# A hybrid state-space and attention layer on one core: turn tied, gate buffers of their own, parities alternated, merge gates loaded early

## The chip, the core and the metric

The kernel runs on one core of one Trainium2 chip. The metric is device time in microseconds (us), the time of one execution of the program on that core. Below, PE is the TensorE, PEld its weight loads, DVE the VectorE, ACT the ScalarE, POOL the GpSimd, and SP the SyncE, whose queue issues most DMAs.

## What is computed

One decoder layer on x of 512 tokens by 1024 channels, all in float32. The reference, cut to its course:

```python
h = rms_norm(x, norm_w)
u_s, z_s, q, k, v, z_a, r_s, r_a = split(h @ w_in)
y_s = s5_branch(u_s, ...)                 # diagonal complex state space, GELU, GLU with w_glu
y_s = (y_s * silu(z_s)) @ w_ssm_out
q, k = partial_rope(rms_norm(q)), partial_rope(rms_norm(k))
y_a = dilated_attention(q, k, v)          # 3 head groups, dilations 1, 4, 16; 8 heads of 64 each
y_a = (y_a * silu(z_a)) @ w_attn_out
m = sigmoid(r_s) * y_s + sigmoid(r_a) * y_a
x = x + m @ w_o
```

## The kernel before

Every large product is made of three matmuls (`mm3`, lines 107 to 110): each operand is split into a high and a low part, and high x high (L108), high x low (L109) and low x high (L110) are summed in a PSUM bank. Weights stream from DRAM: `plan` (lines 112 to 157) lists all pieces of weights in the order of use, `get_w` takes the next and has the two after it loaded; a piece is loaded by SP into `w_raw` (two buffers), ACT makes its high part `w_hi` (L93) and DVE its low part `w_lo` (L95).

The kernel is written as a program of units, in this order:

- The norm of x and its transposition into `hT_hi`, `hT_lo`; then the projections `u` (L300 to L306, L447 to L449). A unit (`cm_unit`, L180) is 24 matmuls into one bank with the tag "pj". Beside them the powers of the state matrix are made on DVE (L307 to L390) and turned by small matmuls into `AT` (L398 to L411): 16 products with the powers' real parts (i = 0), a copy of the half bank by ACT (L405), 16 products for the imaginary parts (i = 1) into the other half of the same bank, their copy, and then `fT` in a bank of its own (L409, L411). From AT come the coefficients `coef` (L253), and from these the transposed W (`w_unit`, L282) and the states X (`x_unit`, L293).
- The gates: `za_unit`, `zs_unit`, `rs_unit`, `ra_unit` (L461 to L483). Each is a projection unit whose bank ACT empties with a tanh into a tile `th` (L458, L474, L482). For rs and ra the tile is stored to DRAM by SP (`gd`, `rad`). `th` has the tag "t2k" (L88), a ring of six buffers of 128 x 512, which it shares with many others, among them the state-space branch's `ysb`, `gs`, `gq`, and later `zl`, `gsum`, `gth`, `rl`, `qsq`, `at`, `vt`, `ral` and `ob`.
- The state-space branch runs in eight groups j (L775 to L785), with the gates' units as fillers between: `ca_unit` (small matmuls cps, L683, then six operations of coefficients on DVE), `m_unit` (16 products kps, L707, each on 64 rows of the array, 16 output partitions; copies to `kt`, eight DMAs by POOL that build the Toeplitz matrix), `y_unit` (products yps, L731 and L738), `g_unit` (transposes yT, L748, GELU, split into `gT_hi`, `gT_lo`). In the kps loop gg runs from 0 to 7, the half of the rows is gg % 2, and the two products of one gg, which add up, follow each other on the same half.
- GLU (L1023 to L1033) and the branch's output projection (L1035 to L1039).
- Attention in four pairs of heads. For each pair: `qk_first` projects q and k of groups 0 and 1 (a `wide_granule`, four quarters of 24 matmuls, L794), their norm and rotation follow on DVE (L823) and POOL (L829 to L834); `qk_turn` (L836) transposes them by PE (L842, two lots of four for each group) through a bank, which ACT (L850) and DVE (L851) empty into high and low parts `qkp`. `scores` (L898) makes the softmax, `values` (L965) transposes the probabilities (L999) and multiplies by V (L985). In the loop (L1070), the granule `qk_second` of the next pair calls `mid` before each of its quarters: the turn of group 0 before quarter 1, that of group 1 before quarter 2, `values` before quarter 3 (counted from 0).
- For the last pair, units ra 3 to 7 fill instead. Then the merge (L1098 to L1110): for each of eight column blocks the gate `ral` is loaded from `rad` (L1103), 12 matmuls are made, and DVE and ACT form `mT` (L1108 to L1110). The residual x is loaded as `xr` (L1112), and two granules with w_o end the kernel.

What is written is not quite what runs: `TileContext(nc, schedule_with_timeline_sim=True)` (L1144) puts the instructions of each engine into an order of its own when the program is built, by its reckoning of when each is ready and by their order in the program; it also places all waits. On the chip each engine then goes through its list in order. So a statement that is moved, or a buffer that is added, can shift the order elsewhere. PSUM is divided into three banks "pj" and five "g" in the first part and four "pj", three "g" and one "o" from L1017 on.

Of the kernel before, what the change touches and what calls it, by code (L numbers as in the profile page):

```python
# [11 lines left out]
F32 = mybir.dt.float32  # L12
# [8 lines left out]
P = 128  # L21
# [6 lines left out]
Q = 16  # L28
# [24 lines left out]
def tile_hybrid_block(ctx: ExitStack, tc: tile.TileContext, x, positions, norm_w, w_in, lam_re, lam_im,  # L53
                      log_dt, b_re, b_im, c_re, c_im, d_skip, w_glu, q_norm_w, k_norm_w, w_ssm_out,
                      w_attn_out, w_o, out, dbg=None):
    nc = tc.nc
    pe, act, dve, pool, sp = nc.tensor, nc.scalar, nc.vector, nc.gpsimd, nc.sync
    dbg = dbg or {}

    cst = ctx.enter_context(tc.tile_pool(name="cst", bufs=1))  # L60
# [2 lines left out]
    tmp = ctx.enter_context(tc.tile_pool(name="tmp", bufs=6))  # L63
# [49 lines left out]
    n_ra = 2  # L113
# [100 lines left out]
    for h in range(2):  # L214
# [10 lines left out]
        for q in range(KT // 2):  # L225
            ps = bank("hps")
# [133 lines left out]
    pw = big.tile([G, 2, 9, N], F32, name="pw", tag="s7a")  # L360
# [31 lines left out]
    H = G // 2  # L392
# [6 lines left out]
    for i in range(2):  # L399
        for k in range(8):  # L400
            for h in range(2):
                o = i * 8 * H + (7 - k) * H
                pe.matmul(ps[64 * h:64 * h + 64, o:o + H], pw[:, i, k], idg[:, h], start=True, stop=True,
                          skip_group_check=True)
        act.copy(AT[:, i, :, 0:8], ps[:, i * 8 * H:(i + 1) * 8 * H].rearrange("p (k g) -> p g k", k=8))  # L405
    ps = bank("ftp")
    for i in range(2):
        for h in range(2):
            pe.matmul(ps[64 * h:64 * h + 64, i * H:(i + 1) * H], pw[:, i, 8], idg[:, h], start=True, stop=True,  # L409
                      skip_group_check=True)  # L410
    act.copy(fT.rearrange("p a g -> p (a g)"), ps[:, 0:2 * H])  # L411

    A4 = cst.tile([P, 2, 2, H], F32, name="A4")
    for i in range(2):
# [37 lines left out]
    sza = cst.tile([P, NP, S], F32, name="sza")  # L452
    gd = dram.tile([2, KT, P, S], F32, name="gd")

    def silu2(dst, ps):

        th = t2k("th")
        act.activation(th, ps, AF.Tanh, scale=0.5)  # L458
        dve.scalar_tensor_tensor(dst, th, 1.0, ps, op0=ALU.add, op1=ALU.mult)

# [9 lines left out]

    def rs_unit(c):
        ps = cm_unit(hT_hi, hT_lo)
        th = t2k("th")
        act.activation(th, ps, AF.Tanh, scale=0.5)  # L474
        sp.dma_start(gd[1, c], th)

# [1 line left out]

    def ra_unit(c):
        ps = cm_unit(hT_hi, hT_lo)  # L480
        th = t2k("th")
        act.activation(th, ps, AF.Tanh, scale=0.5)  # L482
        sp.dma_start(rad[c], th)  # L483

# [214 lines left out]
    def m_unit(j, ca, dg):  # L699

        kt = big.tile([Q, 8, T, Q], F32, name="kt", tag=("s7a", "s7b")[j % 2])
        ps = bank("kps")
        for gg in range(8):
            a, b, h, m = gg % 4, gg // 4, gg % 2, gg // 2
            for c in range(2):
                sl = slice(64 * h, 64 * h + 64)
                pe.matmul(ps[32 * a:32 * a + Q, b * P:(b + 1) * P], BB[sl, 1 + c, 4 * j + m, :], ca[sl, c, m, 1:9, :],  # L707
                          start=c == 0, stop=c == 1, skip_group_check=True, tile_position=(64 * h, 32 * a))
        kv = kt.rearrange("q (b a) k p -> q a b (k p)", a=4)
        for a in range(4):  # L710
            act.copy(kv[:, a], ps[32 * a:32 * a + Q, 0:2 * P].rearrange("q (b m) -> q b m", b=2))  # L711
        pool.tensor_tensor(kt[:, :, T - 1, :], kt[:, :, T - 1, :], dg, op=ALU.add)  # L712

        M = Mb[j % 3]
        for t in range(T):
            pool.dma_start(M[Q * t:Q * t + Q, :, 0:P - Q * t], kt[:, :, t:].rearrange("q g k p -> q g (k p)"))  # L716
        return M
# [349 lines left out]
    ra_unit(n_ra)  # L1067
    qk_turn(2, raw, *QK)

    for hp in range(NP):  # L1070
        Pt = scores(hp, *QK)
        if hp < NP - 1:
            raws = qk_first()

            def mid(kq):
                if kq in (1, 2):
                    qk_turn(kq - 1, raws[kq - 1], *QK)
                if kq == 3:
                    values(hp, Pt, V)

            raw, V_next = qk_second(hp + 1, mid)
            V = V_next
            finv = v0_unit(hp + 1, V)
            qk_turn(2, raw, *QK)
            finv()
        else:
            for c in range(n_ra + 1, KT - 2):
                ra_unit(c)
            values(hp, Pt, V)
            for c in range(KT - 2, KT):  # L1090
                ra_unit(c)
# [6 lines left out]
    for cc in range(KT // 2):  # L1098
        hi, lo = get_w()
        for c2 in range(2):  # L1100
            c = 2 * cc + c2
            th = t2k("ral")
            sp.dma_start(th, rad[c])  # L1103
            ps = ps_p.tile([P, 512], F32, name="pj", tag="pj")
            for k in range(NP):
                mm3(ps, hi[:, k, c2 * P:(c2 + 1) * P], lo[:, k, c2 * P:(c2 + 1) * P], aT[:, 0, k], aT[:, 1, k],
                    k == 0, k == NP - 1)
            dve.scalar_tensor_tensor(th, th, 1.0, ps, op0=ALU.add, op1=ALU.mult)  # L1108
            dve.tensor_tensor(th, th, m1[:, c], op=ALU.add)
            split(mT_hi[:, c], mT_lo[:, c], th, scale=0.5)  # L1110
# [38 lines left out]
```

## Time and profile before

| what | value |
|---|---|
| time, median of 3 runs (lowest to highest) | 743.11 us (741.96 to 743.18) |
| the profiled execution: its time, its span | 742.37 us, 740.6 us |
| mean granted TensorE clock over the span | 0.987 |
| HBM read, written | 68.46 MB, 10.49 MB |
| mean of DMA over the span | 111 GB/s |

The profile is of one execution. Its page has busy times by engine, the span in slices, the DMA queues, the chain of work that ended last, and the costliest groups of instructions: line, engine, operation, output<-inputs, shapes, count, then busy time, the mean of one in ns, the idle time of the engine just before them, and what ended that idle time. The timeline lists instructions in order with start and duration in us, and in brackets the idle time before one and its releaser. The table of windows gives busy times in stretches, and under PEclk the clock that TensorE was granted. An engine's idle time is loss only where that engine sets the pace.

### The profile page before, as it was taken

What the parts mean: (1) busy time and instruction counts of PE and PEld (TensorE: products, weight loads), DVE (VectorE), ACT (ScalarE), POOL (GpSimd) and SP (SyncE); (2) the same over time, 40 slices, a digit from 0 to 9 for tenths busy, and PEclk for the clock granted to TensorE, in tenths of its full rate; (3) what the DMA queues carried; (4) which work ended last, traced back from release to release, by engine and by line L of the source; (5) the groups of instructions that cost most, each with busy time, mean ns of one, the idle gap of its engine ahead of it and who ended that gap; (6) DMA issues with size and microseconds to landing.
All of it is one profiled execution on the core that took longest, in us unless ns stands there. A gap on an engine that the chain in (4) does not pass through costs nothing.

```text
span 740.6 us, 12691 instructions
## 1 busy us (share of the span) xinstructions
PE 699.8 (94%) x4821; PEld 572.7 (77%) x4821; DVE 454.2 (61%) x912; ACT 314.8 (43%) x631; POOL 193.9 (26%) x346
## 2 busy tenths in 40 slices
PE   2789999999999898999999999999999989998997
PEld 2778878789877686888889888787778767887886
DVE  6859746989755743673426669647663765464742
ACT  6434543423244564431244465437344643543310
POOL 3426720421122522540002316012412232120000
PEclk9999999999999999999999999999999999999999
DMA  8334654554454644555332322222302230327441
GB/s 203 102 100 129 170 115 104 141 144 120 117 118 106 119 117 129 171 171 170 86 96 80 101 82 85 58 85 58 96 20 86 58 115 12 106 97 240 131 142 57
DMA packets 137213, 82.14 MB, mean 111 GB/s; under 512 B 32696, under 2 KB 125632, under 8 KB 137024
## 3 DMA queue, kind: packets, MB, share of 16 engines
q1 hardware_dynamic: 135088, 78.96, 37.5%
q0 software_dynamic: 2048, 2.36, 2.3%
q8 instruction: 38, 0.62, 0.4%
q14 instruction: 23, 0.19, 0.1%
q10 hardware_dynamic: 16, 0.00, 0.0%
HBM read 68.46 MB, written 10.49 MB: 107 GB/s over the span
## 4 chain that ended last, share of the span: by engine, by line
PE 88%; ACT 4%; DMA 3%; SPq 2%; DVE 2%; issue 0%; ACTq 0%; DVEq 0%
PE pj L108 24%; PE pj L110 24%; PE pj L109 24%; PE ptp L999 2%; DMA w_raw<-in_w_in_dram 2%; PE ot L985 2%; PE kps L707 1%; DMA ral<-rad 1%; PE yps L731 1%; PE yps L738 1%; PE xps L293 1%; PE wps L282 1%; PE sps L929 1%; ACT w_hi L93 1%; PE qtp L842 1%; SPq L426 1%
## 5 line engine op out<-in xcount | busy, mean ns | idle before, releaser
L93 ACT ACTIVATE w_hi<-w_raw 128x1024 fp32r<-128x1024 f32 x100 | 106.0, 1061 | 233.2 <-PE pj L109 133.7
L95 DVE TENSOR_TENSOR w_lo<-w_raw,w_hi 128x1024 fp32r<-128x1024 f32 x98 | 123.7, 1262 | 120.1 <-ACT w_hi L93 119.5
L108 PE MATMUL pj<-hT_hi,w_hi 128*128 128x512 f32 (+1 forms) x344 | 133.1, 390 | 7.8 <-ACT th L474 5.6
L109 PE MATMUL pj<-hT_lo,w_hi 128*128 128x512 f32 (+1 forms) x344 | 132.5, 386 | 4.1 <-DVE hT_lo L236 4.1
L110 PE MATMUL pj<-hT_hi,w_lo 128*128 128x512 f32 (+1 forms) x344 | 132.4, 386 | 0.8 <-DVE w_lo L95 0.8
L109 PE MATMUL pj<-w_lo,hT_hi 128*128 128x512 f32 (+1 forms) x288 | 106.5, 370 | 0.0
L108 PE MATMUL pj<-w_hi,hT_hi 128*128 128x512 f32 (+1 forms) x288 | 106.5, 371 | 0.0
L110 PE MATMUL pj<-w_hi,hT_lo 128*128 128x512 f32 (+1 forms) x288 | 106.0, 371 | 0.0
L108 PEld LDWEIGHTS pj<-hT_hi,w_hi 128*128 128x128 f32 x344 | 65.0, 190 | 22.8 <-ACT th L474 6.8
L109 PEld LDWEIGHTS pj<-hT_lo,w_hi 128*128 128x128 f32 x344 | 65.4, 190 | 17.5 <-DVE hT_lo L236 4.9
L110 PEld LDWEIGHTS pj<-hT_hi,w_lo 128*128 128x128 f32 x344 | 65.5, 190 | 14.4 <-DVE w_lo L95 1.0
L108 PEld LDWEIGHTS pj<-w_hi,hT_hi 128*128 128x128 f32 x288 | 54.0, 188 | 10.1 <-issue 0.2
L110 PEld LDWEIGHTS pj<-w_hi,hT_lo 128*128 128x128 f32 x288 | 54.0, 188 | 10.0
L109 PEld LDWEIGHTS pj<-w_lo,hT_hi 128*128 128x128 f32 x288 | 54.0, 188 | 9.8
L908 ACT ACTIVATE Pt<-Pt,st 128x256 f32<-128x256 f32 (+1 forms) x64 | 31.0, 491 | 18.7 <-DVE st L906 18.7
L829 POOL TENSOR_TENSOR rt<-qraw,tC 128x256 f32<-128x256 f32 x12 | 14.3, 1190 | 87.7 <-DVE qraw L823 87.4
L712 POOL TENSOR_TENSOR kt<-kt,dg 16x128 f32<-16x128 f32 x8 | 5.6, 702 | 116.8 <-ACT kt L711 116.8
L716 POOL DMA_DIRECT2D dd<-kt x64 | 33.8, 537 | 2.4 <-POOL kt L712 2.4
L938 POOL COPY sw<-st 32x4 f32<-32x4 f32 x64 | 12.0, 188 | 73.1 <-ACT Pt L908 70.4
L851 DVE SCALAR_TENSOR_TENSOR qkp<-qtp,wcol,qkp 128x512 fp32r<-128x512 f32 (+1 forms) x32 | 23.0, 745 | 13.2 <-ACT qkp L850 13.1
L850 ACT ACTIVATE qkp<-qtp,wcol 128x512 fp32r<-128x512 f32 (+1 forms) x32 | 20.8, 686 | 15.7 <-PE qtp L842 10.4
L108 PE MATMUL pj<-gT_hi,w_hi 128*128 128x512 f32 x64 | 24.9, 391 | 2.6 <-ACT th L482 2.6
(267 smaller groups left out, 1306.5 us busy)
## 6 DMA issues: line engine op xcount, KB each, us to landing
w_raw<-in_w_in_dram SPq DMA_DIRECT2D x40, 512.0 KB
w_raw<-in_w_in_dram SPq DMA_DIRECT2D x112, 128.0 KB
w_raw<-in_w_glu_dram SPq DMA_DIRECT2D x8, 512.0 KB
w_raw<-in_w_ssm_out_dram SPq DMA_DIRECT2D x8, 512.0 KB
w_raw<-in_w_o_dram SPq DMA_DIRECT2D x8, 512.0 KB
x_all<-in_x_dram SPq DMA_DIRECT2D x4, 512.0 KB
ud<-uT SPq DMA_DIRECT2D x8, 256.0 KB
Uj<-ud SPq DMA_DIRECT2D x8, 256.0 KB
```

Source lines behind the costliest of these rows:

```text
L93: act.activation(hi, src, AF.Copy, scale=scale)
L95: e.tensor_tensor(lo, src, hi.bitcast(F32), op=ALU.subtract)
L108: pe.matmul(o, lh, rh, start=first, stop=False, skip_group_check=True)
L109: pe.matmul(o, lh, rl, start=False, stop=False, skip_group_check=True)
L110: pe.matmul(o, ll, rh, start=False, stop=last, skip_group_check=True)
L716: pool.dma_start(M[Q * t:Q * t + Q, :, 0:P - Q * t], kt[:, :, t:].rearrange("q g k p -> q g (k p)"))
L829: pool.tensor_tensor(t1, rh[:, :, :, 0:16], cv.broadcast_to([P, NB * 2, 2, 16]), op=ALU.mult)
L850: act.activation(hi, ps[sl], AF.Copy, scale=w)
L851: dve.scalar_tensor_tensor(lo, ps[sl], w, hi.bitcast(F32), op0=ALU.mult, op1=ALU.subtract)
L908: act.activation(o, o, AF.Exp, bias=nm, scale=-1.0, accum_out=st[:, kind, 1, h, b:b + 1])
L985: pe.matmul(o, v, pts[h][:, (2 * i + k) * P:(2 * i + k + 1) * P], start=first, stop=kind == 1 and b == NB - 1 and k == 1, skip_group_check ...
L999: pe.transpose(ps[:, (2 * i + k) * P:(2 * i + k + 1) * P], Pt[:, h, kind, 2 * bb + i, k * P:(k + 1) * P], ident)
```

## The change

- A small class `pe` records the last matmul or transpose that was traced, and `queued()` opens a block whose PE instructions are ordered behind it (an edge that sets the order on PE and adds no semaphore). The turn of group 1 in `mid` stands in such a block, so its transposes come after the last matmul of the granule's second quarter.
- The gates' tanh tiles get a tag "th" with two buffers of their own; ra units 3 to 7 stay on "t2k".
- In the making of AT, all small products, those of `fT` too, stand ahead of the three copies; `fT` is copied first.
- In `m_unit` the loops are turned so that the half of the rows alternates from one product to the next.
- The gates `ral` of column blocks 0 and 1 are loaded into the "th" buffers after the scores of the last pair of heads, ahead of the last five ra units.

```diff
+    def queued():
+        return tc.issue_after(last[0].ins)
...
-        act.copy(AT[:, i, :, 0:8], ps[:, i * 8 * H:(i + 1) * 8 * H].rearrange("p (k g) -> p g k", k=8))
-    ps = bank("ftp")
+    pf = bank("ftp")
     for i in range(2):
         for h in range(2):
-            pe.matmul(ps[64 * h:64 * h + 64, i * H:(i + 1) * H], pw[:, i, 8], idg[:, h], start=True, stop=True,
+            pe.matmul(pf[64 * h:64 * h + 64, i * H:(i + 1) * H], pw[:, i, 8], idg[:, h], start=True, stop=True,
                       skip_group_check=True)
-    act.copy(fT.rearrange("p a g -> p (a g)"), ps[:, 0:2 * H])
+    act.copy(fT.rearrange("p a g -> p (a g)"), pf[:, 0:2 * H])
+    for i in range(2):
+        act.copy(AT[:, i, :, 0:8], ps[:, i * 8 * H:(i + 1) * 8 * H].rearrange("p (k g) -> p g k", k=8))
...
+    def gate_tile():
+        return tmp.tile([P, 512], F32, name="th", tag="th", bufs=2)
...
-        th = t2k("th")
+        th = gate_tile()
...
-        th = t2k("th")
+        th = gate_tile() if c <= n_ra else t2k("th")
...
-        for gg in range(8):
-            a, b, h, m = gg % 4, gg // 4, gg % 2, gg // 2
-            for c in range(2):
-                sl = slice(64 * h, 64 * h + 64)
-                pe.matmul(ps[32 * a:32 * a + Q, b * P:(b + 1) * P], BB[sl, 1 + c, 4 * j + m, :], ca[sl, c, m, 1:9, :],
-                          start=c == 0, stop=c == 1, skip_group_check=True, tile_position=(64 * h, 32 * a))
+        for a0 in (0, 2):
+            for b in range(2):
+                for c in range(2):
+                    for h in range(2):
+                        a, m = a0 + h, 2 * b + a0 // 2
+                        sl = slice(64 * h, 64 * h + 64)
+                        pe.matmul(ps[32 * a:32 * a + Q, b * P:(b + 1) * P], BB[sl, 1 + c, 4 * j + m, :],
+                                  ca[sl, c, m, 1:9, :], start=c == 0, stop=c == 1, skip_group_check=True,
+                                  tile_position=(64 * h, 32 * a))
...
-                if kq in (1, 2):
-                    qk_turn(kq - 1, raws[kq - 1], *QK)
+                if kq == 1:
+                    qk_turn(0, raws[0], *QK)
+                if kq == 2:
+                    with queued():
+                        qk_turn(1, raws[1], *QK)
...
         else:
+            for c in range(2):
+                rals[c] = gate_tile()
+                sp.dma_start(rals[c], rad[c])
             for c in range(n_ra + 1, KT - 2):
                 ra_unit(c)
...
-            th = t2k("ral")
-            sp.dma_start(th, rad[c])
+            if c in rals:
+                th = rals[c]
+            else:
+                th = t2k("ral")
+                sp.dma_start(th, rad[c])
```

More of the change, by code (lines that the diff above doesn't have):

```diff
@@ L56, in tile_hybrid_block, with matmul, transpose @@
     nc = tc.nc
-    pe, act, dve, pool, sp = nc.tensor, nc.scalar, nc.vector, nc.gpsimd, nc.sync
+    act, dve, pool, sp = nc.scalar, nc.vector, nc.gpsimd, nc.sync
+    last = [None]
+    class pe:
+        @staticmethod
+        def matmul(*a, **k):
+            last[0] = nc.tensor.matmul(*a, **k)
+        @staticmethod
+        def transpose(*a, **k):
+            last[0] = nc.tensor.transpose(*a, **k)
+    def queued():
+        return tc.issue_after(last[0].ins)
     dbg = dbg or {}
@@ L472, in rs_unit @@
         ps = cm_unit(hT_hi, hT_lo)
-        th = t2k("th")
+        th = gate_tile()
         act.activation(th, ps, AF.Tanh, scale=0.5)
@@ L480, in ra_unit @@
         ps = cm_unit(hT_hi, hT_lo)
-        th = t2k("th")
+        th = gate_tile() if c <= n_ra else t2k("th")
         act.activation(th, ps, AF.Tanh, scale=0.5)
@@ L1068, in tile_hybrid_block @@
     qk_turn(2, raw, *QK)
+    rals = {}
     for hp in range(NP):
```

## The prediction

> **What bounds the kernel now.** I read the page first, then the groups of TensorE (PE) with the idle time before each, then the table of windows for the granted clock, then the timeline around each idle stretch.
>
> ```profile
> span 740.6 us, 12691 instructions
> PE 699.8 (94%) x4821; PEld 572.7 (77%) x4821; DVE 454.2 (61%) x912; ACT 314.8 (43%) x631; POOL 193.9 (26%) x346
> ```
>
> PE is busy for 699.8 of 740.6 us, and no other engine comes near. The change takes no matmul away, so it can only win from the 40.8 us in which PE is idle, or from time in which PE runs at a lower clock.
>
> ```profile
> L108 PE MATMUL pj<-hT_hi,w_hi 128*128 128x512 f32 (+1 forms) x344 | 133.1, 390 | 7.8 <-ACT th L474 5.6 <-ACT V L882 1.4 <-ACT w_hi L93 0.8
> L842 PE MATMUL qtp<-ident,qraw 128*128 128x128 f32 x96 | 12.9, 274 | 3.5 <-DVE qkp L851 3.5
> L999 PE MATMUL ptp<-ident,Pt 128*128 128x128 f32 x120 | 20.2, 306 | 1.1 <-DVE qkp L851 1.0
> ```
>
> The reader sees who ends PE's waits: the tanh of the merge gate (L474, 5.6 us), and the evictions of turned q and k (L851, 3.5 and 1.0 us). The rest of the idle time is named below, place by place; the start of the kernel, which the change leaves alone, has most of what remains.
>
> ```profile
> core 0: us, PE busy (x) PEld busy (x) DVE busy (x) ACT busy (x) POOL busy (x), PEclk, DMA share, GB/s
> 56.36:59.77 3.41, 3.41 (x17) 2.73 (x14) 3.41 (x7) 1.69 (x3) 2.49 (x5) 0.50 0.58 163
> 244.09:247.50 3.41, 3.37 (x8) 2.69 (x9) 3.38 (x5) 0.63 (x1) 2.08 (x4) 0.50 0.69 135
> 286.00:289.41 3.41, 3.41 (x15) 2.84 (x16) 2.01 (x3) 1.27 (x2) 2.76 (x2) 1.00 0.81 210
> 537.64:541.05 3.41, 3.41 (x17) 2.42 (x17) 2.04 (x4) 1.27 (x2) 0.00 (x0) 0.50 0.17 49
> 609.32:612.73 3.41, 3.38 (x15) 2.40 (x15) 1.94 (x3) 1.35 (x3) 0.00 (x0) 0.50 0.21 64
> 681.00:684.41 3.41, 3.41 (x10) 2.67 (x9) 3.41 (x5) 1.26 (x2) 0.00 (x0) 0.50 0.67 191
> 684.41:687.82 3.41, 3.41 (x17) 2.81 (x16) 3.41 (x7) 0.33 (x1) 0.00 (x0) 1.00 0.86 265
> ```
>
> This view holds what the groups hide. Five windows of 3.41 us show a granted clock of 0.50, and each comes right after one of the idle stretches. In them PE counts as fully busy, but the same matmuls go by at about half the pace: 10 in the window at 681.00 against 17 in the next one, 8 in the one at 244.09 against 15 in the one at 286.00, where one takes 3.41/15 = 0.23 us. Seven matmuls lost out of 15 to 17 are 7/16 of 3.41 us, 1.5 us; half the window, 1.7 us, is the most. I take 1.6 us for each. So a stall of 2 us here costs 3.6 us.
>
> **The change part by part.**
>
> *The copies of AT (L405) behind all their matmuls.*
>
> ```profile
> 54.14 1.06 ACT L93 ACTIVATE w_hi<-w_raw 128x1024 fp32r<-128x1024 f32 x1 [5.52 <-DMA w_raw<-in_w_in_dram]
> 55.10 0.35 ACT L405 COPY AT<-atp 128x256 f32<-128x256 f32 x1
> 55.51 1.24 PE L403 MATMUL atp<-ident,pw 64*64 64x32 f32 x32 [2.44 <-ACT AT L405]
> 66.11 1.04 PE L282 MATMUL wps<-ident,ab 128*128 128x128 f32 x8
> 65.06 0.68 DVE L263 TENSOR_TENSOR ab<-ab 128x512 f32<-128x512 f32 x1
> 66.30:80.00 13.70, 13.70 (x68) 11.10 (x66) 12.74 (x19) 6.66 (x10) 9.11 (x6) 1.00 0.55 139
> ```
>
> The second half of the powers waits for the copy of the first half out of the same bank; that copy stands in ScalarE's queue behind a weight split which waits for its DMA. With both halves ahead of the copy, PE no longer waits at 55.51 for ScalarE: 2.44 us, and the half-clock window at 56.36 with it, 1.6. That is 4.0. The copies are only moved; ScalarE sits idle for 5.52 us there, and it covers them. What is late next is the first transpose of W at 66.11: its data came from VectorE at 65.06+0.68 = 65.74, 0.4 us earlier. PE would now come to it at 62.1. If the order stays and the data come no sooner, 3.6 of the 4.0 come back; but the next projection's weights are there to be multiplied, and the second half of AT is copied earlier too. Ends 0.4 and 4.0; I take 4.0, since in the last row, the 13.7 us behind that point, PE is busy throughout beside a VectorE at 12.74: the order on PE has found other work each time.
>
> *Own buffers for the gates' tanh.*
>
> ```profile
> L108 PE MATMUL pj<-hT_hi,w_hi 128*128 128x512 f32 x23 | 9.2, 400 | 0.0
> L474 ACT ACTIVATE th<-pj x8: 578/580/605, 206.0 to 279.0; 128x512 f32<-128x512 f32 x8
> 205.72 0.38 ACT L742 COPY ysb<-yps 128x256 f32<-128x256 f32 x1 [4.95 <-PE yps L738]
> 217.78 0.63 ACT L755 ACTIVATE gq<-gs 128x512 f32<-128x512 f32 x1
> 218.31 0.58 ACT L474 ACTIVATE th<-pj 128x512 f32<-128x512 f32 x1
> 218.94 0.50 PE L108 MATMUL pj<-hT_hi,w_hi 128*128 128x512 f32 x1 [1.59 <-ACT th L474]
> ```
>
> The first row counts the window 187.1 to 205.9: 23 of the 24 L108 matmuls of three gate units (8 each) are done, yet the first tanh of a gate runs at 206.0, although ScalarE had been idle for 4.95 us. So the engine isn't what is short. Each tanh follows the first write of the tiles that stand before it in the program in the same tag "t2k" (ysb, then gs and gq at 217.78): six buffers are handed out in program order. Three PSUM banks fill up, and PE waits. With a tag of its own the tanh can run when its unit ends. Stalls of 5.6 us on L474 go, and 2.65 us on L482 at the end of the stage (below); of the windows, the one at 244.09 goes, 1.6. At most 9.8 us. What is late next is the GELU of the last group:
>
> ```profile
> 282.27 0.60 PE L748 MATMUL yT<-ident,ysb 128*128 128x128 f32 x4
> 288.71 1.22 DVE L97 SCALAR_TENSOR_TENSOR gT_lo<-gq,gT_hi 128x512 fp32r<-128x512 f32 x1 [0.70 <-ACT gT_hi L93]
> 286.00 0.50 PE L108 MATMUL pj<-gT_hi,w_hi 128*128 128x512 f32 x1 [2.65 <-ACT th L482]
> ```
>
> The GLU stage starts at 286.00 and wants the last slice of gT 22 matmuls later, at 291.1; the slice is ready at 288.71+1.22 = 289.93, 1.1 us ahead. PE would come 9.8 us sooner. If the chain of the state-space groups, which runs through VectorE, gains nothing, PE waits for 8.7 of them and 1.1 is won; if the chain moves with PE, all. I take 7.5, near the upper end: the three stalls on L474 lie inside the chain's own periods, and two more banks offer 2 x 21 matmuls, 9.7 us of work, that don't touch the last slice. The gates' stores to DRAM keep their place on SP; a buffer of the new pair is wanted again two units later, 2 x 24 x 0.23 = 11 us.
>
> *The first two merge gates loaded early.*
>
> ```profile
> 669.27 0.34 SPq L1112 DMA_DIRECT2D xr<-in_x_dram  x1
> 669.66 0.73 SPq L1103 DMA_DIRECT2D ral<-rad  x1
> 679.61 1.36 DVE L1108 SCALAR_TENSOR_TENSOR ral<-ral,pj 128x512 f32<-128x512 f32 x2 [7.73 <-DMA ral<-rad]
> 680.35 0.50 PE L108 MATMUL pj<-aT,w_hi 128*128 128x512 f32 x1 [2.19 <-DVE ral L1108]
> ```
>
> Their loads are issued 0.4 us after the whole residual x and land 10 us later; four banks fill, and PE waits 2.19 us, then has the window at 681.00. Now they stand on SP ahead of the weight loads and stores of the last five gate units; they wait for nothing that is still to be computed, so nothing behind them is held up. 2.19+1.6 = 3.8. Late next are gates 2 and 3, still behind x: they land about 680 and are wanted when bank 3 of the next round is, two units of 12 matmuls (12 x 0.23 = 2.8 us) after PE's last work at 680.35-2.19 = 678.2, at 683.8. So 2.2 to 3.8; I take 3.8.
>
> *The turn of group 1 tied.*
>
> ```profile
> L108 PE MATMUL pj<-w_hi,hT_hi 128*128 128x512 f32 x16 | 6.3, 395 | 0.0
> 531.77 0.74 POOL L834 TENSOR_TENSOR qraw<-rt,rt 128x256 f32<-128x256 f32 x1
> 532.48 1.47 PE L842 MATMUL qtp<-ident,qraw 128*128 128x128 f32 x12
> 535.72 0.66 PE L842 MATMUL qtp<-ident,qraw 128*128 128x128 f32 x4 [1.76 <-DVE qkp L851]
> 537.40 0.93 PE L999 MATMUL ptp<-ident,Pt 128*128 128x128 f32 x4 [0.48 <-DVE qkp L851]
> ```
>
> The first row counts 521.3 to 532.6: 16 matmuls of a kind, 48 in all, two quarters of the granule, stand ahead of the turn at 532.48. So the turn already comes two quarters later than the tie asks for, because GpSimd rotates group 1 until 532.51. A bound from below changes nothing here: 0. The stall of 1.76+0.48 and the window at 537.64 stay, and so does their twin at 609.32. If a new order spreads the turns, as much as 2 x (2.24+1.6) = 7.7 is won; the other end is a rival below.
>
> *Parities in the Toeplitz products.*
>
> ```profile
> 178.51 1.02 PE kps L707 x32
> 204.58 1.09 PE yps L738 x64
> L707 PEld LDWEIGHTS kps<-ab,dd 64*16 64x16 f32 x256 | 7.1, 92 | 3.9 <-issue 3.1 <-PE pj L109 0.4
> ```
>
> Both rows stream 4,096 columns (32 x 128, 64 x 64) on 64 rows of the array; L738 already alternates the halves for every product, and isn't faster (1.09 against 1.02). So 0, the nearer end; the ends are 8 x 0.07 = 0.6 slower and, at twice the pace, 8 x 0.51 = 4.1 faster. [...]
>
> **Sum.** 4.0+7.5+3.8 = 15.3. The profiled execution took 742.37 us (span 740.6 and 1.8 around it); 742.4-15.3 = 727.1. It lies 0.7 under the median of the runs shown, 743.11, and within them. I predict 727.
>
> **Rivals.**
>
> *The tie puts the turn at the head of PE's queue, right behind the second quarter.* Then PE stands from 532.6-48 x 0.23 = 521.5 until the rotation's end at 532.51: 11.0 us, and a half-clock window, 1.6; the stall at the end goes, 3.8. That is 8.8 for each of two head pairs, 17.6 in all: 727.1+17.6 = 744.7, and with AT at its lower end 748.3. It decides from a lead of 9.9 us over the rotation's end: 2 x (9.9+1.6-3.8) = 15.4, all that the rest wins. Against it: the turn has so far followed its data by an instant (532.51, 532.48), and a tie only says "not before". Chance 0.10.
>
> *The tanh stays late, or PE meets gT instead*: 7.5 is lost, 734.6. For it: the slice of gT is only 1.1 us ahead, and its chain is as long as before. Against it: ScalarE's idle 4.95 us, and the work in two more banks. Chance 0.20.
>
> *The clock windows don't go with the stalls.* The window at 286.00 follows the longest stall, 2.65 us, and shows 1.00; so a stall alone doesn't decide, and other waits may trip other windows. The three windows counted are lost, 4.8: 731.9. Chance 0.10. [...]
>
> *The turns spread as well*: 727.1-7.7 = 719.4. Chance 0.12.
>
> *Nothing gained*, the waits only change places: 742. Chance 0.05.
>
> **How the numbers follow.** The forecast, 727 (723 to 733 with its own unknown ends), has 0.43. A measurement of this kernel tells about 0.2%, 1.5 us, from no change. Faster: 0.43+0.20+0.10+0.12 = 0.85; same 0.05; slower 0.10. The range 718 to 738 leaves out the slower rival, the one without gain, and a little of the tails.
>
> **What would show it.** Right: no wait of PE on AT L405, th L474, th L482 or ral L1108; tanh L474 first at about 195, 11 us earlier than now; the granted clock 1.00 in the stages around the gates; PE's busy time less by about 5 us, its idle time by about 10. Unchanged: the 1.76 before the turn, kps at 1.02. Wrong: a new wait of PE on gT_lo L97, on ab L263 or on qraw L834, or a half-clock window where there was none.

## The result and the profile after

The changed kernel took 735.31 us (median of 4 runs, 734.08 to 736.28), the kernel before beside it 743.14 (741.96 to 743.52): 0.989 of the time, with a 95% interval of 0.986 to 0.992. It is faster by 7.8 us. I had 727 as the likeliest, from a gain of 15.3 us, so about half of it came. The profiled execution took 734.36 us.

The page after, its head:

```profile
span 732.6 us, 12680 instructions
PE 699.6 (95%) x4821; PEld 574.2 (78%) x4821; DVE 457.1 (62%) x912; ACT 314.6 (43%) x631; POOL 191.7 (26%) x346
```

PE is busy for as long as before (699.6 against 699.8), although I had expected 5 us less. All 8 us came out of its idle time. The waits of PE after, most costly first (engine, tile, its line, what it waited for, us in all, times, longest):

```profile
PE hps L67 <- DVE x_all L239: 10.4, 1, 10.4
PE qtp L67 <- DVE qkp L874: 3.5, 2, 1.8
PE xps L63 <- DMA Uj<-ud: 3.4, 1, 3.4
PE pj L63 <- DVE hT_lo L251: 3.0, 3, 1.7
PE nps L67 <- DMA nw<-in_norm_w_dram: 2.3, 1, 2.3
PE pj L63 <- DVE w_lo L110: 1.6, 2, 0.9
PE pj L63 <- ACT V L905: 1.4, 3, 0.5
PE pj L63 <- ACT w_hi L108: 1.0, 1, 1.0
PE pj L63 <- ACT gs L776: 1.0, 1, 1.0
```

(All matmuls stand at L63 now and all transposes at L67, the lines of the recording class.) The waits on AT, on the gates' tanh and on `ral` are gone, as forecast. Two are new, and neither is among those that I named: 3.37 us for the load of Uj, and 0.99 us for `gs` (L776), at the start of GLU. The turn's 1.76 us in two head pairs stayed.

By the starts and ends of the projection units the 8.0 us split like this:

| stretch, from one unit's end or start to the next | before | after | difference |
|---|---|---|---|
| start to the end of the first three units | 42.41 | 44.47 | +2.1 |
| to the end of the first `za` unit (AT, W, Uj) | 48.41 | 50.51 | +2.1 |
| to the start of GLU (state space, gates, kps) | 195.18 | 189.21 | -6.0 |
| to the start of the third head pair's V unit | 261.61 | 260.09 | -1.5 |
| to the start of the fourth's | 71.90 | 71.30 | -0.6 |
| to the start of the last product (ra 3 to 7, merge) | 73.45 | 69.37 | -4.1 |
| to the end | 47.6 | 47.6 | 0.0 |

Not every row is the change's doing. The code of the first row is the same in all fourteen kernels, and the row takes 42.4 to 45.6 us in their profiles; the fourth and the fifth hold no edit of PE's work but the tie, and take 260.1 to 264.6 and 69.9 to 72.8; of the two profiles here, the fourth row has one window at a granted clock of 0.50 before (537.64) and none after, the fifth one in each (609.32 and 605.70). So these three differences can't be put down to the change, and here they cancel. Left are +2.1 at AT, -6.0 in the stretch of the gates and -4.1 in the merge. It also means that times from the start of two profiles can't be set beside each other as they are: all that follows the first row stands 2.1 us later in the profile after.

### The profile page after: what moved, and what is told of

Its sections match the earlier page's. It is cut to its first block, busy times and chain, and to the rows that moved or that the text cites. A ratio compares the mean times of both kernels' runs of the same rounds, so it can differ in the third digit from the quotient of the medians.

```text
span 732.6 us, 12680 instructions
## 1 busy us (share of the span) xinstructions
PE 699.6 (95%) x4821; PEld 574.2 (78%) x4821; DVE 457.1 (62%) x912; ACT 314.6 (43%) x631; POOL 191.7 (26%) x346
## 4 chain that ended last, share of the span: by engine, by line
PE 87%; DMA 4%; ACT 3%; DVE 3%; SPq 2%; issue 1%; ACTq 0%
PE pj L63 71%; DMA w_raw<-in_w_in_dram 3%; PE sps L63 3%; PE yps L63 3%; PE ot L63 2%; PE ptp L67 2%; PE kps L63 2%; PE xps L63 1%; PE qtp L67 1%; DMA Uj<-ud 1%; ACT w_hi L108 1%; SPq L442 1%; PE wps L67 1%; ACT qkp L873 1%; DVE w_lo L110 1%
## 5 line engine op out<-in xcount | busy, mean ns | idle before, releaser
L63 PE MATMUL pj<-hT_lo,w_hi 128*128 128x512 f32 (+1 forms) x344 | 132.9, 387 | 3.0 <-DVE hT_lo L251 3.0
L63 PE MATMUL pj<-hT_hi,w_hi 128*128 128x512 f32 (+1 forms) x344 | 132.8, 389 | 2.4 <-ACT V L905 1.4
L63 PE MATMUL pj<-hT_hi,w_lo 128*128 128x512 f32 (+1 forms) x344 | 132.4, 386 | 1.6 <-DVE w_lo L110 1.6
L63 PE MATMUL pj<-w_hi,hT_hi 128*128 128x512 f32 (+1 forms) x288 | 106.5, 372 | 0.0
L63 PE MATMUL pj<-w_lo,hT_hi 128*128 128x512 f32 (+1 forms) x288 | 106.5, 370 | 0.0
L63 PE MATMUL pj<-w_hi,hT_lo 128*128 128x512 f32 (+1 forms) x288 | 106.0, 371 | 0.0
L63 PEld LDWEIGHTS pj<-hT_lo,w_hi 128*128 128x128 f32 x344 | 66.0, 192 | 16.2 <-DVE hT_lo L251 3.9
L63 PEld LDWEIGHTS pj<-hT_hi,w_hi 128*128 128x128 f32 x344 | 65.5, 192 | 16.5 <-ACT V L905 2.1
L63 PEld LDWEIGHTS pj<-hT_hi,w_lo 128*128 128x128 f32 x344 | 65.9, 192 | 15.4 <-DVE w_lo L110 2.3
L63 PEld LDWEIGHTS pj<-w_hi,hT_hi 128*128 128x128 f32 x288 | 54.1, 188 | 10.0 <-issue 0.2
L63 PEld LDWEIGHTS pj<-w_hi,hT_lo 128*128 128x128 f32 x288 | 54.0, 188 | 10.0
L63 PEld LDWEIGHTS pj<-w_lo,hT_hi 128*128 128x128 f32 x288 | 54.0, 188 | 9.8
L277 POOL TENSOR_TENSOR ab<-dd,AT 128x512 f32<-128x512 f32 x16 | 23.0, 1446 | 11.6 <-DVE ab L278 11.6
```

The lines of the kernel that those rows point to most:

```text
L63: last[0] = nc.tensor.matmul(*a, **k)
L277: eng.tensor_tensor(tv, a2.unsqueeze(2).broadcast_to(sh), ai, op=ALU.mult)
```

## The experiments

The kernels, each with the time and its ratio to the kernel before on the same chip, which took 741.73 to 743.06 us there:

| kernel | time, us (lowest to highest) | of before's, 95% interval |
|---|---|---|
| AT edit alone | 746.05 (743.08 to 749.08) | 1.0047 (1.0023 to 1.0071) |
| gates' buffers alone | 734.63 (730.77 to 735.42) | 0.9875 (0.9846 to 0.9903) |
| early merge gates alone | 741.65 (739.29 to 744.26) | 0.9989 (0.9966 to 1.0012) |
| after, kps order as before | 734.01 (732.52 to 735.52) | 0.9875 (0.9851 to 0.9899) |
| after, AT as before | 732.43 (728.71 to 734.19) | 0.9846 (0.9818 to 0.9874) |
| after, kps and AT as before | 733.07 (730.37 to 733.93) | 0.9864 (0.9840 to 0.9889) |
| after without the tie | 735.88 (734.52 to 736.13) | 0.9898 (0.9858 to 0.9938) |
| after, one split first | 734.14 (731.49 to 735.73) | 0.9873 (0.9836 to 0.9911) |
| after, Uj early | 736.49 (733.83 to 738.01) | 0.9908 (0.9880 to 0.9936) |
| after, kps as before, tables late | 731.49 (729.61 to 732.56) | 0.9851 (0.9823 to 0.9879) |

Two more kernels, for the kps order alone, have one time each and serve by their traces.

### The making of AT: alone, and taken back

My theory after the result (A): PE's gain at AT was lost on the way to Uj, and more than that. The rival (B): the AT edit is worth its 4 us, and the loss in that stretch has another cause. First the kernel before with the AT edit alone, then the kernel after without it (the edit is shown in part; the copy that is taken away stands inside the loop over i):

```diff
-        act.copy(AT[:, i, :, 0:8], ps[...])
-    ps = bank("ftp")
+    pf = bank("ftp")
...
+    for i in range(2):
+        act.copy(AT[:, i, :, 0:8], ps[...])
```

> The kernel before with the edit of AT alone. Theory A (the edit wins its wait and loses more behind it): PE's wait on AT L405 at 55 us and its half-clock window go (4.0 us), but the products of X wait for DMA Uj<-ud near 80 us (3.4 us and a half-clock window of 1.6), and in all the stretch up to 190 us loses about 8: 745 to 749 us. Theory B (that wait comes from the gates' own buffers, which change the ring that Uj shares): no wait on Uj, 739 us.

> The changed kernel with the making of AT as before. Theory A: the wait on AT comes back (2.4 us and a half-clock window of 1.6), the wait on Uj and what goes with it disappears (8 us): 731.5 us. Theory B: the wait on AT comes back and that on Uj stays: 739.5 us.

The edit alone made the kernel slower, by 3.5 us, and the kernel after has a median 2.9 us lower without it (732.43 against 735.31, with intervals that overlap), so A holds. The rows show the stretch from the end of the first three units to that of the first `za` unit: before, the edit alone, after, and after with the old making:

```profile
42.41:90.82 48.41, 45.97 (x351) 37.27 (x351) 35.56 (x52) 20.48 (x38) 27.09 (x20) 0.96 0.58 148
```

```profile
45.59:97.12 51.53, 46.39 (x350) 37.36 (x351) 34.80 (x51) 20.65 (x38) 25.80 (x20) 0.97 0.56 141
```

```profile
44.47:94.98 50.51, 46.27 (x351) 37.39 (x351) 34.47 (x51) 20.64 (x38) 26.76 (x20) 0.97 0.55 139
```

```profile
42.56:91.03 48.47, 45.99 (x351) 37.27 (x351) 35.53 (x52) 20.46 (x38) 27.07 (x20) 0.96 0.56 141
```

The second number is the length: 48.4 and 48.5 us with the old making, 51.5 and 50.5 with the new. Over all profiles, the five with the old making give 48.4 to 49.7 (mean 48.9), the six with the new one and no other edit in this stretch 50.5 to 52.4 (mean 51.5). So the edit costs 2.6 us, where I had a gain of 4.0.

Part of where it goes is seen on VectorE. In the timeline before, the split `w_lo` of the seventh unit is begun at 59.07; after, the same split comes after tables of the scan:

```profile
59.07 1.21 DVE L95 TENSOR_TENSOR w_lo<-w_raw,w_hi 128x1024 fp32r<-128x1024 f32 x1
```

```profile
60.50 1.05 DVE L621 TENSOR_TENSOR scn<-A 128x32 f32<-128x32 f32 x1
...
64.35 2.08 DVE L110 TENSOR_TENSOR w_lo<-w_raw,w_hi 128x1024 fp32r<-128x1024 f32 x1
```

Its high part was done at 57.28+1.06 = 58.34 by the next row (ScalarE, after), so the split stood 6.0 us behind products of the coefficients, tables of the scan and adds of the coefficients; before, it stood 2.2 us behind its high part. Then the chain goes over the two `w_raw` buffers to SP's queue, where the load of Uj (75.56) stands right behind a weight load (75.14) that waits for the split begun at 73.90 and done at 73.90+1.22 = 75.12, and over the load itself to PE:

```profile
57.28 1.06 ACT L108 ACTIVATE w_hi<-w_raw 128x1024 fp32r<-128x1024 f32 x1
```

```profile
66.46 0.37 SPq L189 DMA_DIRECT2D w_raw<-in_w_in_dram  x1
...
75.14 0.37 SPq L189 DMA_DIRECT2D w_raw<-in_w_in_dram  x1
75.56 0.62 SPq L265 DMA_DIRECT2D Uj<-ud  x1
```

```profile
66.49 0.50 PE L63 MATMUL pj<-hT_hi,w_lo 128*128 128x512 f32 x1 [0.87 <-DVE w_lo L110]
82.66 1.34 PE L63 MATMUL xps<-Uj,W 128*64 128x64 f32 x32 [3.37 <-DMA Uj<-ud]
```

Before, Uj was issued at 74.03 and PE, which came to it at 80.07, had no wait:

```profile
74.03 0.62 SPq L250 DMA_DIRECT2D Uj<-ud  x1
80.07 1.15 PE L293 MATMUL xps<-Uj,W 128*64 128x64 f32 x31
```

Counted from the end of the first three units, the load was issued at 31.6 us before and at 31.1 after: it came no later, but PE came to it 2.8 us sooner, at 34.8 in place of 37.7, and waited. The products of X then began 0.5 us later than before, and from there to the end of the stretch it took 12.3 us in place of 10.7, with the window at 83.46, 3.41 us at a granted clock of 0.50, in it. These two make the 2.1 us of this pair. So what PE won at AT it lost again before Uj, whose load the edit didn't bring forward, and the clock window behind the wait came on top. Three more kernels ask which link of the chain holds the load where it is.

### One split first

After, with the order on VectorE changed for one split: the scan tables and the adds of the coefficients are queued behind it (`lo_ins` lists the splits, so 6 is the seventh). The order on PE is that of the kernel after.

```diff
+        with tc.issue_after(lo_ins[6].ins):
             dve.tensor_tensor(dst, dst, tv, op=ALU.add)
...
+        with tc.issue_after(lo_ins[6].ins):
             scan_tables()
```

> The kernel after, with VectorE's scan tables (L621 to L628) and the adds of the coefficients (L278) queued behind the weight split w_lo of the seventh projection unit; the order on TensorE is the same. Theory A (the AT edit lost its gain because the tables, ready sooner, went ahead of w_lo, 58.3 to 64.35, and so the next weight loads and the load of Uj came late): w_lo at about 60.5, no wait of 0.87 on it, the weight load at 66.46 about 4 us sooner, the wait of 3.37 on Uj gone or under 1, the half-clock window behind it gone; 735.3 - 3 to 6 = 729 to 732. Theory B (Uj is late by its own buffer or by the store that it reads): the wait on Uj stays at 3 us or more, 735.

```profile
60.48 2.08 DVE L110 TENSOR_TENSOR w_lo<-w_raw,w_hi 128x1024 fp32r<-128x1024 f32 x1
70.55 1.21 DVE L110 TENSOR_TENSOR w_lo<-w_raw,w_hi 128x1024 fp32r<-128x1024 f32 x1
73.88 1.22 DVE L110 TENSOR_TENSOR w_lo<-w_raw,w_hi 128x1024 fp32r<-128x1024 f32 x1
```

```profile
82.99 1.98 PE L63 MATMUL xps<-Uj,W 128*64 128x64 f32 x32 [4.65 <-DMA Uj<-ud]
```

Theory A was right on the first link only. The split came at 60.48, and PE's wait of 0.87 went; but the two splits after it stood behind the same tables, the last of them at 73.88 against 73.90 in the kernel after, so Uj was issued at 75.54, as in the kernel after (75.56). PE came sooner and waited longer, 4.65 us: the wait of 3 us or more that B forecast, though not shown to be for B's reason. At 734.14 the time can't be told from the kernel after.

### Uj loaded early

After, with the first two Uj loaded as soon as their source is stored, into the gates' buffers, which lie idle then:

```diff
     for j in range(3):
         u_unit(j, first[j][1])
+    early = {j: load_u(j, tmp.tile([P, 512], F32, name="Uj", tag="th", bufs=2)) for j in range(2)}
```

> The kernel after, with the loads of the first two Uj right behind the stores of the first three projection units, into the two buffers of the gates' tanh, which lie idle until then. Theory A (Uj is late because its load stands on SP's queue behind a weight load, which waits for the split w_lo at 73.90): no wait on Uj at 82.7, no half-clock window at 83.46; 735.3 - 3.4 - 1.6 = 730, or 732 if the third Uj comes late next. Theory B (what the AT edit takes off one wait comes back at the next, whatever stands there): a wait of 3 us or more somewhere else before the first V unit, or the Uj loads hold up the weight loads behind them on SP; 735.

```profile
66.01 0.66 PE L67 MATMUL wps<-ident,ab 128*128 128x128 f32 x4 [0.45 <-DVE ab L278]
68.61 0.65 PE L67 MATMUL wps<-ident,ab 128*128 128x128 f32 x4 [1.94 <-DVE ab L278]
```

```profile
96.29 0.38 PE L63 MATMUL wcp<-ident,wd 1*128 1x1 f32 x2 [2.04 <-POOL wd L551]
97.52 0.55 PE L63 MATMUL wcp<-ident,wd 1*128 1x1 f32 x2 [0.85 <-POOL wd L551]
```

The wait on Uj went, and what came is close to B: no single wait of 3 us, but 0.45 and 1.94 us on VectorE's coefficients and 2.04 and 0.85 on GpSimd, 5.3 in all. The stretch itself fell to 48.4 us, as with the old making, but the one behind it, to GLU, took 193.2 in place of 189.2, and the time stayed (736.49). The edit also changes the order on PE and GpSimd, so it doesn't isolate the load; it shows that an early Uj alone wins nothing. VectorE is the next candidate: in the kernel after it is busy for 21.88 of 21.91 us from the start of the split at 56.74 to the end of the one at 77.44, in the row's third pair of numbers. PE is busy for 21.04 of them as well, so the row alone decides nothing:

```profile
56.74:78.65 21.91, 21.04 (x98) 16.56 (x97) 21.88 (x36) 10.20 (x14) 13.95 (x11) 1.00 0.46 127
```

### The tables later

So the last test takes work out of this stretch of VectorE: the scan tables go behind the tenth unit's split, the coefficients' adds behind the seventh's as above. The kps order is that of before.

```diff
+        with tc.issue_after(lo_ins[9].ins):
             scan_tables()
```

> The kernel after with the Toeplitz products in the order of before, the adds of the coefficients (L278) behind the split w_lo of the seventh unit, and the scan tables (L615 to L628) behind the split of the tenth; the order on TensorE is that of the kernel after with the old Toeplitz order, which took 734.0 and waited 4.1 us on Uj. Theory A (VectorE, busy without a gap from 56.7 to 78.6, is what the stretch hangs on; the tables in it delay three splits, and with them the weight load ahead of Uj on SP's queue): Uj issued at about 71 in place of 75.5, the wait on Uj under 1 us, no half-clock window at 80 to 87, 727 to 730. Theory B (with VectorE relieved the wait goes to another place, as it did when Uj was loaded early): a wait of 3 us or more before the first V unit, 734.

```profile
71.48 0.37 SPq L190 DMA_DIRECT2D w_raw<-in_w_in_dram  x1
71.90 0.62 SPq L266 DMA_DIRECT2D Uj<-ud  x1
```

```profile
62.60 1.26 PE L67 MATMUL wps<-ident,ab 128*128 128x128 f32 x8 [0.62 <-DVE ab L280]
79.06 1.15 PE L63 MATMUL xps<-Uj,W 128*64 128x64 f32 x32 [2.21 <-DMA Uj<-ud]
```

Uj is issued at 71.90, near the 71 of A, but 2.0 us of the way from 75.56 is the shorter start of this profile: counted from the end of the first three units it is issued at 29.5 us, against 31.1 in the kernel after and 31.0 in the kernel with the same PE order (after, kps as before). The wait on it is 2.21 us, against 4.1 there. The stretch takes 48.95 us, against 52.1 there and 50.51 in the kernel after; a part of the 52.1 may be a second window at half clock, which no row here shows. That is A in part: the wait was to be under 1 us and the half-clock window behind it to go; it stayed (matmuls 0.43 us apart from 82.00 to 83.28, 0.23 ahead of the wait; a mean granted clock of 0.97 over the stretch). The median, 731.49, is the lowest here, against 734.01, with intervals that overlap. With the tables moved the stretch is as long as with the old making of AT (mean 48.9); the edit costs nothing there any more, nor does it win, since the load of Uj, 79.06-71.90 = 7.2 us from issue to use, is then what PE meets. So the order on VectorE is shown, from one profile of each, to hold back the load by 1.5 us; the rest of the loss hangs on the load's own time and on the clock window.

### The gates' buffers alone

Before, with the two buffers of the tag "th" for the tanh of za, zs, rs and the first ra units. Theory A: the waits on the tanh go, and no wait on Uj appears. B: the wait on Uj comes with this edit, since Uj has had its buffer from the same ring.

> The kernel before with the tanh tiles of the gates in two buffers of their own, and nothing else. Theory A: the waits of PE on th L474 and L482 go and no wait on Uj appears: 743.1-7.7 = 735.5 us. Theory B: the wait on Uj comes with this edit: 743 us.

A holds: there is no wait on Uj, and it took 734.63, 7.9 us less than before on the same chip, where A had 7.7. From the end of the first `za` unit to the start of GLU, before and with the buffers alone:

```profile
90.82:286.00 195.18, 186.95 (x1981) 150.46 (x1979) 133.78 (x181) 85.07 (x174) 53.38 (x90) 0.99 0.49 121
```

```profile
94.98:281.75 186.77, 185.43 (x1981) 149.62 (x1978) 131.63 (x178) 82.81 (x172) 52.81 (x89) 1.00 0.50 128
```

That is 8.4 us: PE's idle time there falls from 8.2 to 1.3, the half-clock window at 244.09 goes (the mean granted clock in the rows is 0.99, then 1.00), and no wait on gT takes their place; the 1.3 us are at the start of GLU, where PE waits for `gs`.

### The order of the Toeplitz products

The kernel after with the loop over gg of before. A: the new order itself slows the lots. B: it changes only the time at which they stand.

> The changed kernel with the Toeplitz products in the order of before. Theory A (the alternated order is slower on TensorE itself, 1.24 us from first to last start instead of 0.82 in an unbroken lot): 8 x 0.42 = 3.4 us less, 732 us, and the lots at 0.82 again. Theory B (the longer lots only take up time in which PE would wait anyway): 735 us.

In the same stretch, after and with the old order:

```profile
94.98:284.19 189.21, 187.85 (x1981) 151.57 (x1978) 131.61 (x178) 83.08 (x172) 49.56 (x89) 1.00 0.52 128
```

```profile
94.87:281.68 186.81, 185.46 (x1982) 149.75 (x1979) 131.56 (x178) 82.81 (x172) 52.43 (x89) 1.00 0.50 127
```

The new order costs 2.4 us here, 0.3 for each of the eight lots, and 2.2 in the pair of kernels with the old AT (188.96 and 186.79). That is A, at two thirds of its 3.4 us. The medians, 734.01 against 735.31, show less than that and can't resolve it. Only one of the eight lots stands whole, without other matmuls in between, and two more kernels take its new order apart. The first puts one half of the rows after the other:

```diff
-        for a0 in (0, 2):
+        for h in range(2):
             for b in range(2):
                 for c in range(2):
-                    for h in range(2):
+                    for a0 in (0, 2):
```

> The kernel after, with the Toeplitz products of one half of the rows all ahead of those of the other (the half changes once in 16 products, the 16-column strip with each). Theory A (the change of the half at each product is what slowed the lots): the whole lot takes 0.82 us or less from first to last start, as before. Theory B (what slowed it is that the strip changes with each product and that a sum's second product no longer follows its first): 1.24 us or more, as after.

The second puts one strip of 16 columns after the other:

```diff
         for a0 in (0, 2):
-            for b in range(2):
+            for h in range(2):
                 for c in range(2):
-                    for h in range(2):
+                    for b in range(2):
```

> The kernel after, with the four Toeplitz products of one strip of 16 columns next to each other, but with the two terms of a sum still apart (c outside b). Theory A (the change of the strip at each product is what slowed the lots): a whole lot takes 0.82 us from first to last start, as before. Theory B (the second term of a sum no longer follows its first): 1.24 us, as after.

The whole lot in the timeline before, after, with the halves and with the strips one after the other (from its first start to its last end, 0.27 us more than to its last start, by which the theories count):

```profile
178.44 1.09 PE L707 MATMUL kps<-ab,dd 64*16 64x128 f32 x32
```

```profile
183.89 1.51 PE L63 MATMUL kps<-ab,dd 64*16 64x128 f32 x32
```

```profile
184.18 1.51 PE L63 MATMUL kps<-ab,dd 64*16 64x128 f32 x32
```

```profile
186.44 2.40 PE L63 MATMUL kps<-ab,dd 64*16 64x128 f32 x32
```

The times are 1.09 before, 1.51 after, 1.51 with the halves one after the other, 2.40 with the strips one after the other (whose kernels took 734.32 and 744.08 us); with the old order put back into the kernel after the lot takes 1.09 again. So it isn't the half: with it fixed for eight products the lot is as slow as with it alternating. It isn't the change of the strip either, as A of the last test had it: keeping the strip for four products made it worse, and by far more than B's 1.51. What the fast order has and none of the three others is that the second term of a sum stands right behind its first. That is a description of four orders, not a mechanism; which rule of the array makes it so stays open, and so does why the strips are slower still, since there too one product stands between the two terms.

### The merge gates early, alone

Before, with the first two loads of `ral` ahead of the last gate units, in two buffers of their own.

```diff
+            for c in range(2):
+                rals[c] = tmp.tile([P, 512], F32, name="ral", tag="ral", bufs=2)
+                sp.dma_start(rals[c], rad[c])
             for c in range(n_ra + 1, KT - 2):
```

> The kernel before, with only the first two merge gates' loads issued early, into two buffers of their own. Theory A: the 2.19 us wait on ral L1108 and the half-clock window behind it go, 742.6 - 3.8 = 738.8. Theory B (gates 2 and 3, still loaded behind x, come late next): a wait on ral of 1.6 us stays, 741 to 742.6.

The wait is gone in its trace, as A said, but the time, 741.65 against 741.73, is not 3.8 us less, and its interval ends at -2.5. A likely reason is in two kernels that still have the late loads. PE's wait, first with the AT edit alone, then with the gates' buffers alone:

```profile
685.49 0.50 PE L108 MATMUL pj<-aT,w_hi 128*128 128x512 f32 x1 [1.13 <-DVE ral L1109]
```

```profile
674.24 0.50 PE L108 MATMUL pj<-aT,w_hi 128*128 128x512 f32 x1 [1.14 <-DVE ral L1111]
```

There the same code waits 1.1 us, with no half-clock window behind it (the granted clock is 1.00 over the merge's products in both), where the profile of before had 2.19 and a window (0.50 at 681.00). The merge's products take 33.6 us in that profile, 30.9 in these two, and 29.5 in every kernel with the early loads. So by the traces the edit is worth 1.4 to 4.1 us in the merge, by the run, and the profile that I priced it from was a dear draw; the medians of the edit alone show no gain. In the kernel after, the order made at build time puts the two loads far ahead of where they are written: SP issues them at 409.8 and 417.2 us, and the merge begins at 655.61.

### The tie, taken away

> The kernel after without the tie of group 1's turn. Theory A (the turn stands behind the rotation anyway): the same time, 735.3, the waits of 1.76 and 0.48 on qkp L874 in both head pairs as with the tie. Theory B (without it the turn goes to the head of TensorE's queue and waits there for the rotation): a wait on qraw of several us in each of two head pairs, 740 or more.

A: 735.88 us, and the turn stands where it stood, with the wait that it has after. By tile, the matmuls and transposes come on PE in the same order, from first to last, as with the tie, so the tie changes nothing:

```profile
532.34 1.47 PE L67 MATMUL qtp<-ident,qraw 128*128 128x128 f32 x12
535.58 0.66 PE L67 MATMUL qtp<-ident,qraw 128*128 128x128 f32 x4 [1.77 <-DVE qkp L874]
```

### Both losing edits taken back

> The kernel after, with the order of the Toeplitz products and the making of AT as before: only the gates' buffers, the early merge gates and the tie are left of the change. If the two edits that are taken back cost 2.0 to 2.9 and 1.3 to 2.4 us, each on its own: 735.3 - 3.3 to 5.3 = 730 to 732. If the later work only waits elsewhere: 734 to 735.

At 733.07 it lies between the 730 to 732 of the sum and the 734 to 735 of the rival, so neither is shown, and it is not below the kernel with only AT as before (732.43). These runs can't tell the two, or the one with late tables, from each other. The two lowest, 731.49 and 732.43, beat the kernel before by 1.2 to 1.8%; their intervals end below the 0.989 of the kernel after, but overlap with its own.

## Why the prediction was right, and where it was not

*The total: inside the range, partly by luck.* The 735.3 us lie inside 718 to 738, but outside the 723 to 733 that I gave the forecast with its own unknown ends. They lie next to the 734.6 of the rival in which the gates' 7.5 us are lost, and that rival did not come. What is missing of the 15.3 us, 7.5, is missing because AT cost time where I had a gain, and the Toeplitz products where I had 0.

*The gates' own buffers, 7.5: right, in mechanism and size.* They were worth 8.4 us in the stretch and 7.9 by the medians; the first tanh of an rs gate now follows its unit by 0.8 us (200.95, unit's end 200.18; I had said about 195), and the rival in which PE meets gT did not come: the 0.99 us at GLU's start end with the copy `gs`, not with a slice of gT.

*AT, 4.0: the step that failed.* "The order on PE has found other work each time" was argued from a row in which PE is busy for 13.70 us beside a VectorE at 12.74. I read past what it held: PE's later work hangs on a chain over VectorE's splits and SP's queue to the load of Uj, and VectorE's 12.74 of 13.70 left that chain little room to come sooner (this much is argued; shown is that later tables brought the load 1.5 us forward). PE came to Uj 2.8 us earlier, Uj didn't, and behind the wait of 3.37 us came a half-clock window of its own (0.50 at 83.46). I had one later wait in mind (W's transposes, at most 3.6 back), not this one, nor that the earlier AT would put tables ahead of the splits. Measured: a loss of 2.6, so 6.6 us off, against 7.5 that are missing in all. A half-clock window where there was none, at 83.46, is among the signs of being wrong that I had named.

*kps, 0 with ends of +0.6 and -4.1: the step failed beyond its end.* I took the pace of yps, which alternates halves, for that of kps; but it says nothing of where a sum's second term stands. A loss of 2.2 to 2.4 us in the stretch.

*Merge gates, 3.8: the mechanism right, the size a draw.* The wait went; 4.1 us in the two profiles, 1.4 between kernels whose late loads cost PE a shorter wait, and no gain that the medians of the edit alone show.

*The tie, 0, and the turn's wait that stays: right.*

*Half-clock windows at 1.6 each: right in price for one window, wrong as something that an edit takes away.* The price fits the window at 83.46: from the start of X to the end of its stretch it took 12.3 us, against 10.7 before. But over all profiles 14 of 50 such stretches of half clock lasted two windows. The window that I subtracted at 56.36 was followed by a new one at 83.46, one at 35.67 stood where before had none (which fits the +2.1 at the start), and that at 537.64 went though its stall didn't. In the rows below, what follows a stall goes with how it lies on the grid of windows. They are windows on the grid of after, and one of before, with the granted clock third from the end:

```profile
530.61:534.02 3.41, 1.65 (x14) 1.34 (x13) 2.05 (x3) 3.14 (x7) 0.11 (x1) 1.00 0.11 28
534.02:537.44 3.42, 2.94 (x20) 1.97 (x20) 2.94 (x5) 2.82 (x6) 0.00 (x0) 1.00 0.54 153
602.29:605.70 3.41, 1.47 (x10) 0.76 (x8) 3.04 (x4) 3.41 (x10) 0.00 (x0) 1.00 0.21 61
605.70:609.11 3.41, 3.10 (x13) 2.36 (x13) 2.22 (x4) 1.63 (x4) 0.00 (x0) 0.50 0.31 93
```

```profile
534.22:537.64 3.42, 1.44 (x9) 0.97 (x10) 3.14 (x5) 3.24 (x9) 0.00 (x0) 1.00 0.38 107
```

The first window holds the whole of the turn's 1.76 us (3.41-1.65), and the one behind it runs at 1.00. At 602.29 the same stall lies so that a part of the next one, 0.48 us long, falls into the same window, 1.94 us in all, and the window behind it runs at 0.50. So it was before, with 1.98. The grid doesn't settle all of it: of the eleven windows in all profiles with 1.76 or 1.77 us of idle time, seven were followed by one at half clock and four were not. Within a profile the starts of the windows at half clock lie whole multiples of 3.413 us apart, to within 0.1 us: before, 55 from 56.36 to 244.09 and 86 from there to 537.64; after, 14 from 35.67 to 83.46 and 153 from there to 605.70. Counted from the start of the span, the two grids lie 0.2 us apart. In the windows above, 1.94 and 1.98 us of idle time out of 3.41 were followed by half clock, and 1.76 was not.

## What to carry to other kernels

Before time on the busiest engine is counted as won, follow what it will need next back to the queue that brings it, and look at the engines on the way: here VectorE was nearly full (12.74 of 13.70), the load of Uj came no sooner, and the earlier start only moved the wait and brought forward work that stood in front of a weight split. Where instructions are put in order when the kernel is built, data that come sooner change the order on engines that the edit never named, so compare the order of the feeders too. And price a stall from more than one profile if it is to be set against a per cent or less: the same code waited 1.1 or 2.2 us, with or without a half-clock window behind it, 1.6 us by my estimate. Times in two profiles are best counted from an event that both have close by.

## What the runs showed of the hardware

- The idle time of PE within one window of the grid, and the granted clock in the next. Over all fourteen profiles, leaving out windows that ran at half clock themselves and those ahead of a profile's first record of the clock (at 15.40 us before, at 18.61 after): all 32 windows with 1.88 us of idle time or more were followed by one at 0.50; of 25 with 1.60 to 1.88 us, 16 were; of 33 with 1.20 to 1.60, two; of 24 with 0.90 to 1.20, none. In the profile of before, the windows from 52.94, 240.68, 534.22, 605.91 and 677.59, with 2.44, 2.13, 1.98, 2.20 and 2.19 us, were followed by 0.50, those from 29.05 and 281.64, with 1.68 and 1.70, by 1.00; in that of after, those from 32.26, 80.05 and 602.29, with 1.73, 2.61 and 1.94, by 0.50, that from 530.61, with 1.76, by 1.00. The stall of 2.65 us at 286.00, which cost no clock before, lay across two windows (1.70 and 0.95 us). Counted from the gaps before each matmul.
- The same behind a window that ran at half clock itself. Of the 64 such windows in the same profiles, leaving out the tails after the last matmul, all 45 with less than 0.25 us of idle time were followed by full clock; 14 of the 19 with more, 0.26 to 2.46 us, were followed by a second one at half clock. After, that at 605.70, with 0.31 us, was followed by full clock.
- A lot of 16 small products with the same operands takes 1.09, 1.51 or 2.40 us by its order alone (before, after, and with the strips one after the other).
